# State-space heads of a hybrid diffusion step: one full-row selection matmul per direction, with the moving tile brought by DMA

## The chip, the cores and the metric

The kernel runs on one core of one Trainium2 chip. The metric is the device time of one execution in microseconds, as the median of several runs. All inputs, weights and results are f32 in HBM. The engines named below are PE (TensorE, matmuls), ACT (ScalarE), DVE (VectorE), POOL (GpSimd) and SP (SyncE, which here issues every DMA).

## What is computed

The reference is one inference step of a two-layer trunk, for 128 context tokens and 256 latent tokens. Layer 0 mixes tokens with a Fourier transform and with attention, layer 1 with a gated linear recurrence (RG-LRU) and with a state-space model of 16 heads (SSD). Each layer ends in a SwiGLU network. The change lies in the state-space heads. For each of two directions and each chunk of 128 tokens the reference computes

```python
acs = jnp.cumsum(dtc * A.reshape(G, Hg), axis=2)
diff = acs[:, :, :, None] - acs[:, :, None, :]
causal = jnp.tril(jnp.ones((Q, Q), dtype=bool))[:, :, None, None]
decay = jnp.exp(jnp.where(causal, diff, -jnp.inf))
cb = jnp.einsum("bcqgn,bckgn->bcqkg", Cc, Bc)
y_diag = jnp.einsum("bcqkg,bcqkgh,bckgh,bckghp->bcqghp", cb, decay, dtc, xc)
...
y_off = jnp.einsum("bcqgn,bcghpn,bcqgh->bcqghp", Cc, h_in, jnp.exp(acs))
```

So for each head, direction and chunk a 128 x 128 matrix exp(acs[q] - acs[k] + log dt[k]) is wanted, masked to one side of the diagonal. There are three chunks: one of context tokens and two of latent tokens.

## The kernel before

Activations lie with channels on partitions and tokens in the free dimension: 128 context tokens, two gap columns that carry the shift, and 256 latent tokens, 386 in all. Weights come from HBM in chunks of eight 128 x 128 blocks (`wr`, 512 KB, four buffers). ACT rounds a chunk to its high part (`wh`), DVE takes the rest (`wl`), and PE makes each product as three matmuls: high by high, high by low and low by high (`mm3`, line 622). The layers' stages follow each other: even mixer, network 0, odd mixer, network 1.

No engine's order is written by hand. All operations are recorded first; then a list scheduler (`schedule`, lines 308 to 456) gives each engine an order, with a cost for each instruction, the number of buffers of each pool, and a limit on how far ahead of the oldest unscheduled operation one may be taken. That limit is the first number of a row of `PARTS` (lines 213 to 218); the odd mixer is the third row. Since ACT, DVE, PE and SP each work through their order as it stands, a waiting instruction holds up all that stand behind it. Helpers record the operations, so that a profile shows lines 529 (ACT), 539 and 552 (DVE), 589 and 593 (PE) and 582 (SP) for nearly all of them, and tiles have to be told apart by name.

`odd_mixer` (line 1109) projects 27 tiles of 128 output channels from the normed input: 27 x 8 x 3 = 648 matmuls of 386 columns on `xh` and `xl`. The order of the tiles is written at line 1112; each is evacuated and worked on as it comes:

- `deltas` (line 1226) makes the step sizes `dt` and the cumulative sums `acs`, transposes `acs` and `nacs` (log dt - acs) to 32 rows (16 heads x 2 directions), and splits each with `both` into high and low parts, `rr` and `nrr`. In these 128-row tiles rows 0 to 63 and rows 64 to 127 hold the same numbers. It also makes `pick` (columns of an identity), `sel` and `ee` (exp(acs), high and low, 64 rows), and the two masks.
- `xs_tile` (line 1338) makes the heads' inputs `xt` and, scaled, `xw`; `states` (line 1368) makes the chunk states `Hc` and stores `news`.
- `ssd` (line 1389) runs twice after every second `xs` tile, for two heads each. For a head it fills one PSUM bank per direction: a matmul of 384 columns brings acs[q] to all 128 partitions, three matmuls of 128 columns add the key's own log dt - acs, and a matmul of 384 columns adds the mask. Direction 0 uses rows 0 to 63, direction 1 rows 64 to 127:

```python
                for d in range(2):
                    ds = slice(64 * d, 64 * d + 64)
                    r = S["pick"][ds, d * 16 + h:d * 16 + h + 1].to_broadcast([64, 128])
                    self.mm(q[d][:, :NC_], r, S["rr"][ds], True, False)
                    for c in range(3):
                        cc = slice(c * 128, (c + 1) * 128)
                        self.mm(q[d][:, cc], S["nrr"][ds, cc], r, False, False)
```

  ACT takes the exponential into `M` (32 in all), DVE adds the directions and multiplies by `cb`. One more matmul of 64 rows and 256 columns (`sel`, `ee`) gives the decay for the state's part, and DVE makes `exs` of it. `M` and `exs` then go through PE with `xt` and `Hc`, and `ysum` holds the head's output.
- `gated` (line 1454) takes SiLU of the `z` tiles (`zw`), multiplies, squares (`sq`) and sums (`ss`); `lru` and `lru_scan` do the recurrence, `gate` (line 1431) makes `gu` and the split pair `mh`, `ml`.

After the 27 tiles the norm of `ysum` is computed (matmuls on `ss`, then `rs`), and the output projection follows: 8 x 12 x 3 = 288 matmuls of 384 columns on `mh` and `ml`, whose first four of twelve row blocks come from `gate`. Exp and Tanh, SiLU and Tanh, GELU and Tanh, Sqrt, and Ln lie in different activation tables; ACT loads one (ACT_TABLE_LOAD) when the next function is not in the present table.

Of the kernel before, what the change touches and what calls it, by code (L numbers as in the profile page):

```python
# [9 lines left out]
F32 = mybir.dt.float32  # L10
F32R = mybir.dt.float32r
I32 = mybir.dt.int32
BF16 = mybir.dt.bfloat16
AF = mybir.ActivationFunctionType
ALU = mybir.AluOpType
# [9 lines left out]
NC_ = NP_ + NS_  # L25
# [45 lines left out]
def constants():  # L71
    c = np.zeros((128, NCON), np.float32)
    c[:, CO["ident"]] = np.eye(128)
    c[:, CO["ones"]] = 1.0
    h = np.arange(128)
    c[:, CO["halves"]][:, 32:34] = h[:, None] // 64 == np.arange(2)[None]

    c[:, CO["lo"]] = h[:, None] <= h[None]
    c[:, CO["up"]] = h[:, None] >= h[None]
    t = np.arange(NS_)  # L80
    pos = np.stack([t // 64, t % 64]).astype(np.float32)
    freqs = (np.float32(10000.0) ** (-np.arange(16, dtype=np.float32) / np.float32(16))).astype(np.float32)
    d = h % 64
    ang = pos[d // 32] * freqs[d % 16][:, None]
    sign = np.where(d % 32 < 16, -1.0, 1.0)[:, None]
    c[:, CO["cos"]] = np.cos(ang)
    c[:, CO["sin"]] = np.sin(ang) * sign
    a = 2 * np.pi * ((d[:, None] * d[None]) % 64) / 64
    same = (h[:, None] // 64) == (h[None] // 64)
    c[:, CO["dft64"]] = np.concatenate([np.where(same, np.cos(a), 0), np.where(same, np.sin(a), 0)], 1)  # L90
    a = 2 * np.pi * ((h[:, None] * h[None]) % 128) / 128
    s = 1 / math.sqrt(128 * 64)
    c[:, CO["dft128"]] = np.concatenate([np.cos(a) * s, -np.sin(a) * s], 1)
    a = 2 * np.pi * ((t[:, None] * t[None]) % 256) / 256
    s = 1 / math.sqrt(256 * 64)
    for k in range(2):
        c[:, CO["dft256" + "ac"[k]]] = np.cos(a[k * 128:(k + 1) * 128]) * s
        c[:, CO["dft256" + "bd"[k]]] = -np.sin(a[k * 128:(k + 1) * 128]) * s
    return c

# [97 lines left out]
class Recorder:  # L200
# [12 lines left out]
    PARTS = (  # L213
        (900, 10, 150, 0.8, 0.25, 60),
        (500, 12, 150, 0.4, 0.15, None),
        (900, 10, 150, 0.4, 0.25, 200),
        (500, 12, 150, 0.4, 0.15, None),
    )

# [239 lines left out]
class Kernel:  # L459
# [649 lines left out]
    def odd_mixer(self):  # L1109
# [114 lines left out]
        S = {}  # L1224

        def deltas(p):

            t = self.slot("dtT")
# [3 lines left out]
            q = self.bank()  # L1232
            for c in range(3):
                self.tp(q[:, c * 128:(c + 1) * 128], t[:, CH[c]:CH[c] + 128])
            v = self.tile("dv", 96, F32, "c")
# [6 lines left out]
            q = self.bank()  # L1242
# [5 lines left out]
            acs = self.tile("acs", 96, F32, "c")  # L1248
# [4 lines left out]
            et = self.tile("et", 96, F32, "c")  # L1253
            self.act(et, tot[:, 0:96], AF.Exp)
            q = self.bank()
            for c in range(3):
                self.tp(q[0:32, c * 128:(c + 1) * 128], acs[:, c * 32:(c + 1) * 32])
            def both(q):

                rr = self.slot("rr", NC_, F32R)  # L1260
                for z in range(2):
                    self.act(rr[64 * z:64 * z + 32], q[0:32, :NC_], AF.Copy)
                self.tt(rr[32:64], q[0:32, :NC_], rr[0:32].bitcast(F32), ALU.subtract)
                self.act(rr[96:128], rr[32:64].bitcast(F32), AF.Copy)
                return rr

            rr = both(q)
            er = self.slot("er", NC_)
            self.act(er[0:32], q[0:32, :NC_], AF.Exp)
            ee = self.slot("ee", NC_, F32R)  # L1270
            self.split_hl(ee[0:32], ee[32:64], er[0:32])

            nacs = self.tile("nacs", 96, F32, "c")
            self.ts(nacs, dt, 2.0 ** -126, ALU.max)
            self.act(nacs, nacs, AF.Ln)
            self.tt(nacs, nacs, acs, ALU.subtract)
            q = self.bank()
            for c in range(3):
                self.tp(q[0:32, c * 128:(c + 1) * 128], nacs[:, c * 32:(c + 1) * 32])
            nrr = both(q)  # L1280
            pick = self.slot("pick", 32, F32R)
            for z in range(4):
                zs = slice(32 * z, 32 * z + 32)
                self.act(pick[zs], self.ident[zs, zs], AF.Copy)

            sel = [self.tile("sel", 1024, F32R, "k") for _ in range(2)]
            for z in range(2):
                for d in range(2):
                    self.act(sel[z][0:64].split(8)[:, :, d * 64:d * 64 + 64],
                             pick[0:64, d * 16 + z * 8:d * 16 + z * 8 + 8].bitcast(F32).unsqueeze(2).to_broadcast([64, 8, 64]), AF.Copy)  # L1290

            mask = []
            for mk in ("lo", "up"):
# [2 lines left out]
                mask.append(t)  # L1296
            dd = self.tile("dd", 96, F32, "c")
            self.tt(dd, dt, de)
            S.update(dd=dd, nrr=nrr, et=et, rr=rr, ee=ee, pick=pick, sel=sel, mask=mask)

        def bc(i, p):
            y = conv(p, self.sm("csw")[:, (8 + i) * 4:(8 + i) * 4 + 4], self.sm("csb")[:, 8 + i:9 + i])
# [86 lines left out]
        def ssd(j):  # L1389

            o = self.bank()
            g = j // 4
            M, ex = {}, {}
            for hb in range(2):
                h = 2 * j + hb
                q = [self.bank() for _ in range(2)]
                for d in range(2):
                    ds = slice(64 * d, 64 * d + 64)
                    r = S["pick"][ds, d * 16 + h:d * 16 + h + 1].to_broadcast([64, 128])
                    self.mm(q[d][:, :NC_], r, S["rr"][ds], True, False)  # L1400
                    for c in range(3):
                        cc = slice(c * 128, (c + 1) * 128)
                        self.mm(q[d][:, cc], S["nrr"][ds, cc], r, False, False)
                for d in range(2):
                    self.mm(q[d][:, :NC_], self.identr, S["mask"][d], False, True)
                    m = self.slot("M", NC_)
                    self.act(m, q[d][:, :NC_], AF.Exp)
                    M[hb, d] = m
                self.tt(M[hb, 0], M[hb, 0], M[hb, 1], ALU.add)
                self.tt(M[hb, 0], M[hb, 0], S["cb"][g])  # L1410
                q = self.bank()
                self.mm(q[:, 0:256], S["sel"][h // 8][0:64, h % 8 * 128:h % 8 * 128 + 128], S["ee"][0:64, 128:384])
                ex[hb] = self.slot("exs", NS_)
                self.tt(ex[hb], q[:, 0:256], S["cs"][g])
            for c in range(3):
                cc = slice(c * 128, (c + 1) * 128)
                for hb in range(2):
                    self.mm(o[hb * 64:hb * 64 + 64, cc], xt[j][:, c * 128 + hb * 64:c * 128 + hb * 64 + 64], M[hb, 0][:, cc],
                            True, c == 0)
                if c:  # L1420
                    for hb in range(2):
                        h = 2 * j + hb
                        self.mm(o[hb * 64:hb * 64 + 64, cc], Hc[c - 1][:, h * 64:h * 64 + 64], ex[hb][:, (c - 1) * 128:c * 128], False, True)
            y = self.slot("ysum", NC_)
            for i in range(2):
                self.stt(y[:, CSEG[i]], ysum[j][:, SEG[i]], skip[:, j:j + 1], o[:, CSEG[i]], ALU.mult, ALU.add)
            ysum[j] = y
# [281 lines left out]
```

## Time and profile before

| | |
|---|---|
| median of 3 runs | 983.16 us (982.57 to 983.31) |
| the profiled execution | 981.94 us |
| its span | 980.2 us, 16154 instructions |
| mean granted TensorE clock | 0.994 |
| busy: PE, DVE, ACT, POOL | 98%, 75%, 51%, 0% of the span |
| DMA | 159.85 MB, mean 163 GB/s |

A group of instructions is shown as line, engine, operation, the tile written and the tiles read (buffer numbers left out), its shapes and its count, then its busy time and the mean of one, then the idle time of the engine just before it with what ended it. Matmuls overlap, so the time of one is longer than the distance between two starts; a PE that is shown as busy may be waiting inside its queue. PEclk is the clock that was granted to TensorE, 1.00 for 2.4 GHz and 0.50 for 1.2 GHz.

### The profile page before, as it was taken

The page shows a single profiled execution, that of the slowest core. Times are in us where ns is not written, and L with a number is a line of the kernel's source. Part 1 is how long each engine was busy: PE and PEld are TensorE (multiplying, and loading weights), DVE is VectorE, ACT ScalarE, POOL GpSimd, SP SyncE. Part 2 cuts the span into 40 slices and gives each one's busy share as a digit, 9 for nine tenths or more (in the row PEclk, how much of TensorE's full clock was granted, in tenths as well). Part 3 has the DMA queues.
Part 4 walks back from the last instruction along what each step waited for, and adds up shares of the span by engine and source line. Part 5 has one row for each costly group of instructions (what it writes and reads, how often), then busy time and mean ns, then how long its engine had stood idle before and what let it go on. Part 6 is the DMA issues. An engine that isn't in the chain of part 4 may idle for free.

```text
span 980.2 us, 16154 instructions
## 1 busy us (share of the span) xinstructions
PE 958.7 (98%) x6190; PEld 916.9 (94%) x6190; DVE 731.0 (75%) x1550; ACT 499.4 (51%) x949; POOL 4.3 (0%) x41
## 2 busy tenths in 40 slices
PE   6999999999999999999999999999999999999998
PEld 4987879999999999999997888899999999999998
DVE  3598765999999999996399799895889555553332
ACT  4569774544333442344278989774444433342221
POOL 0000000000000000000000000000000000000000
PEclk9999999999999999999999999899999999999999
DMA  9983524765666667744321222134643333333340
GB/s 358 362 325 106 180 87 144 286 215 189 214 222 214 217 218 247 253 146 146 127 87 50 80 82 86 50 108 135 242 161 129 129 129 123 116 127 129 131 155 16
DMA packets 47179, 159.85 MB, mean 163 GB/s; under 512 B 5376, under 2 KB 9216, under 8 KB 47104
## 3 DMA queue, kind: packets, MB, share of 16 engines
q1 hardware_dynamic: 47104, 158.84, 46.5%
q8 instruction: 48, 0.79, 0.3%
q14 instruction: 27, 0.22, 0.1%
HBM read 156.45 MB, written 2.37 MB: 162 GB/s over the span
## 4 chain that ended last, share of the span: by engine, by line
PE 87%; ACT 8%; DVE 2%; issue 1%; DMA 1%; SPq 0%; DVEq 0%; ACTq 0%
PE ps L589 85%; PE ps L593 2%; ACT wh L529 1%; DMA ar<-in_ada 1%; ACT L529 1%; ACT xw L529 1%; ACT kk L529 1%; ACT X L529 1%; ACT M L529 0%; SPq L582 0%; ACT cv L529 0%; ACT ex L529 0%; ACT kl L529 0%; ACT th L529 0%; ACT xt L529 0%
## 5 line engine op out<-in xcount | busy, mean ns | idle before, releaser
L529 ACT ACTIVATE wh<-wr 128x1024 fp32r<-128x1024 f32 x191 | 202.0, 1058 | 354.3 <-PE ps L589 242.7
L589 PE MATMUL ps<-xh,wh 128*128 128x386 f32 x1016 | 347.9, 343 | 2.2 <-ACT rstd L529 2.2
L589 PE MATMUL ps<-xl,wh 128*128 128x386 f32 x1016 | 347.7, 342 | 0.0
L589 PE MATMUL ps<-xh,wl 128*128 128x386 f32 x1016 | 346.2, 341 | 0.0
L539 DVE TENSOR_TENSOR wl<-wr,wh 128x1024 fp32r<-128x1024 f32 x191 | 233.2, 1221 | 112.5 <-ACT wh L529 108.4
L589 PEld LDWEIGHTS ps<-xh,wh 128*128 128x128 f32 x1016 | 192.5, 190 | 6.0 <-ACT rstd L529 2.8
L589 PEld LDWEIGHTS ps<-xl,wh 128*128 128x128 f32 x1016 | 192.4, 189 | 3.1 <-issue 2.1
L589 PEld LDWEIGHTS ps<-xh,wl 128*128 128x128 f32 x1016 | 192.2, 189 | 0.9 <-issue 0.3
L552 DVE SCALAR_TENSOR_TENSOR junk<-ar,scb 128x1024 bf16<-128x1024 f32 x112 | 136.5, 1219 | 3.0 <-DMA ar<-in_ada 1.4
L589 PE MATMUL ps<-gh,wh 128*128 128x384 f32 x352 | 118.7, 337 | 0.0
L589 PE MATMUL ps<-gh,wl 128*128 128x384 f32 x352 | 118.5, 337 | 0.0
L589 PE MATMUL ps<-gl,wh 128*128 128x384 f32 x352 | 118.5, 337 | 0.0
L539 DVE TENSOR_TENSOR ft<-ps,rstd 128x386 f32<-128x386 f32 x88 | 48.2, 558 | 52.7 <-PE ps L589 50.5
L589 PEld LDWEIGHTS ps<-gl,wh 128*128 128x128 f32 x352 | 66.1, 188 | 0.0
L589 PEld LDWEIGHTS ps<-gh,wl 128*128 128x128 f32 x352 | 66.1, 188 | 0.0
L589 PEld LDWEIGHTS ps<-gh,wh 128*128 128x128 f32 x352 | 66.1, 188 | 0.0
L589 PE MATMUL ps<-ml,wh 128*128 128x384 f32 x160 | 54.3, 339 | 0.0
L589 PE MATMUL ps<-mh,wl 128*128 128x384 f32 x160 | 54.1, 338 | 0.0
L589 PE MATMUL ps<-mh,wh 128*128 128x384 f32 x160 | 53.3, 339 | 0.0
L529 ACT ACTIVATE xh<-x,G 128x128 fp32r<-128x128 f32 x64 | 26.3, 446 | 23.9 <-DVE x L552 16.8
L529 ACT ACTIVATE gh<-fs 128x384 fp32r<-128x384 f32 x44 | 23.1, 525 | 25.8 <-DVE fs L552 25.7
L552 DVE SCALAR_TENSOR_TENSOR fs<-ft,fs 128x128 f32<-128x128 f32 x88 | 33.3, 414 | 3.7
(226 smaller groups left out, 1044.9 us busy)
## 6 DMA issues: line engine op xcount, KB each, us to landing
wr<-in_wst SPq DMA_DIRECT2D x191, 512.0 KB, 3.3
ar<-in_ada SPq DMA_DIRECT2D x96, 512.0 KB, 4.6
x<-in_x SPq DMA_DIRECT2D x4, 386.0 KB, 9.6
out_y<-x SPq DMA_DIRECT2D x8, 193.0 KB, 2.9
scb<-in_cond SPq DMA_DIRECT2D x2, 512.0 KB, 6.5
lw<-in_lru_w SPq DMA_DIRECT2D x2, 512.0 KB, 4.7
Hc<-in_h SPq DMA_DIRECT2D x2, 256.0 KB, 4.7
out_new_ssd<-news SPq DMA_DIRECT2D x4, 128.0 KB, 1.8
```

What stands on the lines that cost most here:

```text
L529: lambda: nc.scalar.activation(out=R(out), in_=R(in_), func=func, bias=R(bias), scale=R(scale), accum_out=R(accum_out)),
L539: self.dve(out, [a, b], out.free, lambda: nc.vector.tensor_tensor(out=R(out), in0=R(a), in1=R(b), op=op))
L552: lambda: nc.vector.scalar_tensor_tensor(out=R(out), in0=R(a), scalar=R(s), in1=R(b), op0=op0, op1=op1, accum_out=R(accum_out)),
L589: self.rec.add("PE", c / 1e3, [out], [lhsT, rhs], lambda: nc.tensor.matmul(R(out), R(lhsT), R(rhs), start=start, stop=stop), cols=cols)
L593: self.rec.add("PE", 0.109, [out], [in_, ident], lambda: nc.tensor.transpose(R(out), R(in_), R(ident)), cols=2 * in_.shape[0])
```

## The change

A table `selv` of 18 tiles of zeros and ones is made on the host. For a head, its tile `mvt` (128 x 384) is brought by DMA, and a second, small DMA puts four rows of `rr` (the head's cumulative sums: high and low part, both directions) into rows 48 to 51. ACT copies the whole to `mv` in the rounded type. The stationary tile `own` (one per direction) holds log dt - acs of all heads and chunks, high part in rows 0 to 47 and low part in rows 64 to 111, and ones in the rows of its direction's sums. One matmul of 128 rows and 384 columns per head and direction then does what four of 64 rows did. `ee` and `sel` are zero-filled to 128 rows, `rr` is kept once and not doubled, `nrr` is gone, and the scheduler's limit for the odd mixer goes from 900 to 500.

```diff
+def selectors():
+    s = np.zeros((18, 128, NC_), np.float32)
+    for h in range(16):
+        for c in range(3):
+            s[h, [c * 16 + h, 64 + c * 16 + h], c * 128:(c + 1) * 128] = 1.0
+    for d in range(2):
+        s[16 + d, [48 + d, 50 + d], 0:128] = 1.0
+    return s
...
     PARTS = (
         (900, 10, 150, 0.8, 0.25, 60),
         (500, 12, 150, 0.4, 0.15, None),
-        (900, 10, 150, 0.4, 0.25, 200),
+        (500, 10, 150, 0.4, 0.25, 200),
...
-            def both(q):
-
-                rr = self.slot("rr", NC_, F32R)
-                for z in range(2):
-                    self.act(rr[64 * z:64 * z + 32], q[0:32, :NC_], AF.Copy)
-                self.tt(rr[32:64], q[0:32, :NC_], rr[0:32].bitcast(F32), ALU.subtract)
-                self.act(rr[96:128], rr[32:64].bitcast(F32), AF.Copy)
-                return rr
-
-            rr = both(q)
+            rr = self.slot("rr", NC_, F32R)
+            self.act(rr[0:32], q[0:32, :NC_], AF.Copy)
+            self.tt(rr[32:64], q[0:32, :NC_], rr[0:32].bitcast(F32), ALU.subtract)
...
+            self.memset(ee[64:128].bitcast(F32), 0.0)
...
-            self.tt(nacs, nacs, acs, ALU.subtract)
+            steps = self.tile("steps", 96, F32, "c")
             q = self.bank()
-            for c in range(3):
-                self.tp(q[0:32, c * 128:(c + 1) * 128], nacs[:, c * 32:(c + 1) * 32])
-            nrr = both(q)
-            pick = self.slot("pick", 32, F32R)
-            for z in range(4):
+            own = []
+            for d in range(2):
+                v = steps[:, d * 48:d * 48 + 48]
+                ds = slice(d * 16, d * 16 + 16)
+                self.tt(v.split(3), nacs.split(3)[:, :, ds], acs.split(3)[:, :, ds], ALU.subtract)
+                self.tp(q[0:48, d * 128:(d + 1) * 128], v)
+
+                w, t = self.slot("ownt", 128), self.slot("own", 128, F32R)
+                self.dma(w, self.io["selv"][16 + d, :, 0:128])
+                self.act(t, w, AF.Copy)
+                self.act(t[0:48], q[0:48, d * 128:(d + 1) * 128], AF.Copy)
+                self.tt(t[64:112], q[0:48, d * 128:(d + 1) * 128], t[0:48].bitcast(F32), ALU.subtract)
+                own.append(t)
+            pick = self.slot("pick", 32)
+            for z in range(2):
...
             for z in range(2):
+                self.memset(sel[z][64:128].bitcast(F32), 0.0)
...
                 q = [self.bank() for _ in range(2)]
+
+                t, mv = self.slot("mvt", NC_), self.slot("mv", NC_, F32R)
+                self.dma(t, self.io["selv"][h])
+                self.dma(t[48:52], S["rr"].bitcast(F32)[h:64:16])
+                self.act(mv, t, AF.Copy)
                 for d in range(2):
-                    ds = slice(64 * d, 64 * d + 64)
-                    r = S["pick"][ds, d * 16 + h:d * 16 + h + 1].to_broadcast([64, 128])
-                    self.mm(q[d][:, :NC_], r, S["rr"][ds], True, False)
-                    for c in range(3):
-                        cc = slice(c * 128, (c + 1) * 128)
-                        self.mm(q[d][:, cc], S["nrr"][ds, cc], r, False, False)
+                    self.mm(q[d][:, :NC_], S["own"][d], mv, True, False)
...
-                self.mm(q[:, 0:256], S["sel"][h // 8][0:64, h % 8 * 128:h % 8 * 128 + 128], S["ee"][0:64, 128:384])
+                self.mm(q[:, 0:256], S["sel"][h // 8][:, h % 8 * 128:h % 8 * 128 + 128], S["ee"][:, 128:384])
```

The scheduler's new order shows at three places. The rows name line, operation, tile written and tiles read, and size of the output; PSUM banks are `ps`. The first place is PE at one head of the middle of the program; before:

```order
L589 MATMUL ps_6249<-rr_5808,pick_5208 128x384
L589 MATMUL ps_6251<-rr_5808,pick_5208 128x384
L589 MATMUL ps_6249<-pick_5208,rr_5821 128x128
L589 MATMUL ps_6251<-pick_5208,rr_5821 128x128
```

and now, with the masks and the decay selection behind:

```order
L602 MATMUL ps_6382<-mv_6176,own_5240 128x384
L602 MATMUL ps_6388<-mv_6176,own_5247 128x384
L602 MATMUL ps_6382<-mask_5212,identr_71 128x384
L602 MATMUL ps_6388<-mask_5242,identr_71 128x384
L602 MATMUL ps_6396<-ee_5024,sel_5007 128x256
```

The pair of 128-column matmuls stands three times for a head before (`rr_5821` is the tile that the code calls `nrr`), so that eight matmuls have become two.

The second place is SP at the first heads; before, behind the weight chunks that are loaded ahead:

```order
L582 DMA wr_5817<-in_wst 128x1024
L582 DMA wr_5888<-in_wst 128x1024
L582 DMA out_new_ssd<-news_6025 128x256
L582 DMA wr_6165<-in_wst 128x1024
L582 DMA wr_6196<-in_wst 128x1024
L582 DMA out_new_ssd<-news_6228 128x256
```

and now:

```order
L595 DMA wr_5828<-in_wst 128x1024
L595 DMA mvt_5201<-rr_5822 4x384
...
L595 DMA out_new_ssd<-news_6012 128x256
L595 DMA mvt_6027<-in_selv 128x384
L595 DMA mvt_6037<-in_selv 128x384
L595 DMA mvt_6027<-rr_5822 4x384
L595 DMA mvt_6089<-in_selv 128x384
L595 DMA mvt_6037<-rr_5822 4x384
L595 DMA mvt_6104<-in_selv 128x384
L595 DMA wr_6115<-in_wst 128x1024
L595 DMA mvt_6089<-rr_5822 4x384
L595 DMA mvt_6104<-rr_5822 4x384
```

The tables of the first eight heads are loaded earlier, between weight chunks, and their eight small copies stand in one row after the weights; those of the next four stand behind the store of `news`, with a weight chunk between them. The last four heads' come later in the same way.

The third place is ACT after the exponentials of the first heads; before, where the gating (`zw`) begins:

```order
L529 ACTIVATE M_6130<-ps_6039 128x384
L529 ACTIVATE wh_6135<-wr_5705 128x1024
L529 ACTIVATE X_5186<-X_5186 128x128
L529 ACTIVATE X_5186<-X_5186 128x256
L529 ACT_TABLE_LOAD
L529 ACTIVATE zw_6152<-zt_5583 128x128
```

and now:

```order
L542 ACTIVATE wh_6164<-wr_5719 128x1024
L542 ACTIVATE mv_6176<-mvt_6027 128x384
L542 ACTIVATE mv_6182<-mvt_6037 128x384
L542 ACTIVATE mv_6187<-mvt_6089 128x384
L542 ACTIVATE mv_6193<-mvt_6104 128x384
L542 ACTIVATE xt_6201<-ps_6185 128x384
```

The sixteen `zw` now stand in one stretch after the last `M`, where before twelve of them stood ahead of it; and the program's ACT_TABLE_LOADs have become 15 where there were 22.

## Rows read from the trace of the kernel before

**Rows 1.** Busy time by stage (stretch: length, then each engine busy, with instructions)

```profile
core 0: us, PE busy (x) PEld busy (x) DVE busy (x) ACT busy (x) POOL busy (x), PEclk, DMA share, GB/s
493.20:618.40 125.20, 121.06 (x801) 106.44 (x803) 114.55 (x274) 109.97 (x234) 0.00 (x0) 0.98 0.23 76
618.40:642.10 23.70, 23.70 (x144) 21.07 (x145) 19.86 (x42) 19.43 (x35) 0.10 (x1) 0.94 0.17 54
642.10:724.80 82.70, 82.70 (x476) 82.25 (x476) 66.57 (x141) 37.13 (x60) 0.00 (x0) 1.00 0.50 177
```

**Rows 2.** The chain that ended last, in order of time: start, length, what

```profile
213.31 278.91 PE ps L589 x1589
...
616.06 108.73 PE ps L589 x627
```

**Rows 3.** Timeline of PE: start, length, instruction; where the output projection begins

```profile
641.75 0.34 PE L589 MATMUL ps<-xl,wh 128*128 128x386 f32 x1
641.92 0.34 PE L589 MATMUL ps<-xh,wl 128*128 128x386 f32 x1
642.10 0.72 PE L589 MATMUL ps<-cons,ss 128*128 128x1 f32 x6
642.68 0.42 PE L589 MATMUL ps<-mh,wh 128*128 128x384 f32 x1
```

**Rows 4.** Timeline of PE at one head: its selection, then the decay's

```profile
546.54 0.44 PE L589 MATMUL ps<-rr,pick 64*128 64x384 f32 x2
546.82 0.44 PE L589 MATMUL ps<-pick,rr 64*128 64x128 f32 x6
547.10 0.33 PE L589 MATMUL ps<-ee,sel 64*128 64x256 f32 x1
```

**Rows 5.** Busy time by microsecond where the granted clock falls and rises

```profile
614.00:615.00 1.00, 1.00 (x7) 0.93 (x5) 0.91 (x4) 1.00 (x3) 0.00 (x0) 0.60 0.91 336
...
620.00:621.00 1.00, 1.00 (x4) 0.79 (x3) 0.23 (x1) 0.65 (x3) 0.00 (x0) 0.50 0.00 0
621.00:622.00 1.00, 1.00 (x7) 1.00 (x7) 0.95 (x3) 1.00 (x1) 0.00 (x0) 0.99 0.36 123
```

**Rows 6.** Groups of ACT from 493 to 643 us

```profile
L529 ACT ACTIVATE wh<-wr 128x1024 fp32r<-128x1024 f32 x20 | 21.0, 1051 | 4.9 <-PE ps L589 4.9
L529 ACT ACT_TABLE_LOAD x15 | 19.2, 1283 | 0.3
```

**Rows 7.** Timeline of ACT: copies like the new ones and those that go

```profile
513.95 1.96 ACT L529 ACTIVATE rr<-ps 32x384 fp32r<-32x384 f32 x4
516.68 0.94 ACT L529 ACTIVATE rr<-rr 32x384 fp32r<-32x384 f32 x2
...
655.27 1.58 ACT L529 ACTIVATE mh<-ysum 128x384 fp32r<-128x384 f32 x3 [0.69 <-DVE ysum L552]
```

**Rows 8.** Timelines of ACT and DVE where the first pair for the output projection is made

```profile
638.05 0.51 ACT L529 ACTIVATE mh<-gu 128x384 fp32r<-128x384 f32 x1
...
638.98 0.55 DVE L539 TENSOR_TENSOR ml<-gu,mh 128x384 fp32r<-128x384 f32 x1
```

**Rows 9.** DMA issues from 560 to 660 us: KB each, median us from issue to landing

```profile
out_new_ssd<-news SPq DMA_DIRECT2D x2, 128.0 KB, 2.1
out_new_lru<-finals SPq DMA_DIRECT2D x1, 4.0 KB, 2.9
```

**Rows 10.** Timelines of SP (an issue), then ACT (the work that will stand between)

```profile
546.84 0.34 SPq L582 DMA_DIRECT2D out_new_ssd<-news  x1
...
561.74 2.79 ACT L529 ACTIVATE M<-ps 128x384 f32<-128x384 f32 x7
...
568.12 1.07 ACT L529 ACTIVATE xw<-xt,dd 128x64 f32<-128x64 f32 x4
...
571.52 0.79 ACT L529 ACTIVATE X<-X 128x128 f32<-128x128 f32 x2
572.21 1.04 ACT L529 ACTIVATE wh<-wr 128x1024 fp32r<-128x1024 f32 x1
```

More of the change, by code (lines that the diff above doesn't have):

```diff
@@ L1287, in deltas @@
             for z in range(2):
+                self.memset(sel[z][64:128].bitcast(F32), 0.0)
                 for d in range(2):
                     self.act(sel[z][0:64].split(8)[:, :, d * 64:d * 64 + 64],
-                             pick[0:64, d * 16 + z * 8:d * 16 + z * 8 + 8].bitcast(F32).unsqueeze(2).to_broadcast([64, 8, 64]), AF.Copy)
+                             pick[0:64, d * 16 + z * 8:d * 16 + z * 8 + 8].unsqueeze(2).to_broadcast([64, 8, 64]), AF.Copy)
             mask = []
@@ L1298, in deltas @@
             self.tt(dd, dt, de)
-            S.update(dd=dd, nrr=nrr, et=et, rr=rr, ee=ee, pick=pick, sel=sel, mask=mask)
+            S.update(dd=dd, own=own, et=et, rr=rr, ee=ee, sel=sel, mask=mask)
         def bc(i, p):
@@ L1627 @@
         x=(128, KC, NT), cond=(2, D), smalls=(128, NSM), consts=(128, NCON), wst=(N_CHUNKS, 128, NBLK * 128),
-        ada=(96, 128, 1024), ck=(2, 128, 128), cv=(128, 256), lru_w=(128, 16, 128), h0=(128, 1024))
+        ada=(96, 128, 1024), selv=(18, 128, NC_), ck=(2, 128, 128), cv=(128, 256), lru_w=(128, 16, 128), h0=(128, 1024))
     outs = dict(y=(128, KC, NT), new_k=(128, 2, 128), new_v=(128, 2, 128), new_lru=(128, 8), new_ssd=(128, 1024))
@@ L1646 @@
     A["consts"][:] = constants()
+    A["selv"][:] = selectors()
     s = A["smalls"]
```

## The prediction

> **What bounds the kernel now.** I read the stages first, then the chain, then the timelines inside the one stage that the change touches. The chain of waits is PE alone for 278.91 us from 213.31 and again for 108.73 us from 616.06 [rows 2]; between 493 and 616 it breaks into short pieces on ACT, DVE and PE. So outside the odd mixer nothing that the change does can shorten the end, and inside it there are two halves. From 493.2 (its input is normed) to 618.4 (the last `M` has been made) ACT is busy for 109.97 of 125.20 us and DVE for 114.55, while the 121.06 of PE contain waits inside its queue [rows 1]: here the three engines hold each other. From about 621 on PE issues one matmul every 0.17 to 0.18 us [rows 3], and 476 of them fill 82.70 us from 642.10 on [rows 1]. The first matmul of the output projection starts at 642.68, directly behind the projection's last and the six on `ss` [rows 3]. Nothing behind this point changes, so the whole question is how much earlier it comes. PE reaches it at 642.1 by its own work. The other side of the door is ACT and DVE: the first pair `mh`, `ml` is made at 638.05 and 638.98, and so is there at 639.5 [rows 8]. They are only about 3 us ahead of PE. Whatever PE gains beyond that is given back unless ACT gains too.
>
> **The selection on PE.** For one head the eight half-row matmuls run from 546.54 to 547.10, where the next kind starts: 0.56 us [rows 4]. They are replaced by two of 128 rows and 384 columns, at the 0.175 us of a full matmul [rows 3]: 0.35 us. Sixteen heads: 16 x 0.21 = 3.4 us less PE work. Bounds: 0, if the eight cost no more than their columns, and 3.4; I take 3.4, since the row is of this very sequence. One transpose fewer (three of `nacs` become two of `steps`) is below 0.2 us. The decay's matmul gets 128 rows at unchanged 256 columns: I cost it at nothing, since the distance of two matmuls goes with columns in all rows above; if it cost a tenth of its 0.33 us [rows 4], that would be 0.5 us over the heads.
>
> The Trainium skill speaks against this term: TensorE: Matmul & The Clock Gate, Part 3 (packing small matmuls), says that matmuls on different row groups run side by side. By that rule the eight run as four pairs, 384 + 3 x 128 = 768 columns, the same as two full matmuls of 384, and the term would be 0. The trace agrees on the pairing, and not on the sum: 0.56 us against 0.35.
>
> **The clock.** In the microsecond from 614 the granted clock falls to half (1.2 GHz) and is back in that from 621 [rows 5]. Just before, PE had issued heads 12 to 15: mostly half-row selections, with a pause. At most 6.6 us at half speed have cost 3.3 us; as PE also waited for ACT there, I take 2.0. Ends: 0 (the dip comes again) and 3.3. That full-row matmuls keep the clock up is plausible and not shown by any row; a new dip elsewhere is the third rival.
>
> **ACT.** Added: 16 copies `mv` of 128 x 384 into the rounded type. The nearest rows are three `mh` copies of that shape, 1.58 us for three, and the two `rr` copies of 32 rows, 0.94 for two [rows 7]: 0.53 and 0.47 each, so 7.5 to 8.4; I take 7.8. Two small `own` copies add about 0.8, by the length of the `rr` copies; the full-width `own` copies and the zero fills on POOL fall into the network before, where PE alone is the chain. Removed: three of the four `rr` copies out of PSUM (1.96 for four) and both copies of `rr` [rows 7], 2.4 us. The new order loads an activation table seven times less: 7 x 1.283 = 9.0 us [rows 6]; all fifteen loads between 493 and 643 stand in the stretch at issue. Sum: 7.8 + 0.8 - 2.4 - 9.0 = -2.8 us for the stage.
>
> Where that falls matters more. By the new order twelve `zw` and six squares (18 x 0.4, the distance of two `M` [rows 10]), four weight copies (4 x 1.04 [rows 10]), one table load and some 5 us of the last heads' own inputs move behind the last `M`: about 18 us of ACT, and as much goes from ahead of it, the seven loads among that. The last head therefore comes much earlier, and ACT's work from there to the first `mh` grows from 15 us (of the 19.43 in rows 1 those ahead of 638.05) to 33, about as much as PE has left there: 168 projection matmuls where there were 96, x 0.175 = 29.5 us, and the last heads' products. Up to the first `mh` ACT's total work is then only about 0.7 us less than before, because work that stood behind that point has moved ahead of it. DVE loses one split of `rr` and gains two small ones of `own`: 0.
>
> **The queues.** SP gets 34 more issues at 0.34 us [rows 10], 12 us of a queue that mostly waits for buffers. The bytes, 16 x 197 KB, are nothing at a DMA share of 0.23 [rows 1]. The new waits are the matter. For heads 0 to 7 only the small copies are due; eight issues behind one another and a landing of 2.1 to 2.9 us [rows 9] end before ACT has done its other work there. For heads 8 to 11 the chain starts when ACT has made `news`: store, two table loads, a landing, small copy, a landing, so 0.34 x 4 + 2.1 + 2.5 = 6 us for the first, and about 10 for the fourth, which has a weight chunk and two more landings in front. Meanwhile ACT has 1.07 (`xw`) + 0.79 (`X`) + 4 `mv` at 0.5 + 2 x 1.04 (`wh`) + eight `M` at 0.4 [rows 10] = 9 us. That fits, with 3 us to spare for the first. The buffers of the later tables have to be free in time as well, which no row shows. I add 0, with 0 to 8 as ends.
>
> **The sum.** PE's side: 642.1 - 3.4 - 2.0 = 636.7. ACT and DVE's side: the first pair at 639.5 - 0.7 = 638.8. The later side decides: the projection starts some 3.8 us earlier. The profiled execution took 981.94 us, which gives 978.1; the median of the runs is 1.2 us higher, so 979.3 is forecast.
>
> **The rivals.** *Slower: the small copies are late.* ACT stands at `mv` while SP waits for a buffer or a landing; behind ACT's copy all `M` wait, and behind SP's the next weight chunks. It decides from a hold of more than 3 us in the chain of heads 8 to 11. With 4 us lost at each of the two later groups of four heads, the gain is gone and 4 us more: 987. For it: three dependent transfers replace none, on a queue that also carries `news` and weights. Against: SP is idle most of this time, and the first half of the heads is loaded ahead.
>
> *The tail becomes ACT's.* With 33 us behind the last `M`, three more microseconds of waiting there than the 4.3 that ACT has after 618.4 (23.70 - 19.43 [rows 1]) undo most of it: 982.
>
> *The clock falls in another stretch.* The heads now stand closer together, with few projection matmuls between them. Then the 2.0 are not won and up to 3.3 lost once: PE's side is 642.1 - 3.4 - 0 + 1.3 = 640, and the time 981 to 982.
>
> *The selection is worth nothing on PE*, if the pairs are as good as full rows, which also covers that the change does not do what it says: 642.1 - 2.0 = 640.1, and 981.2.
>
> *More is won.* ACT stood idle for 15.2 us of the 125.2 before the last `M` [rows 1], part of it waiting for PE (4.9 us at `wh` alone [rows 6]). If that shrinks by 4 us with the shorter selections, both sides move: 975.
>
> **How the numbers follow.** About 0.2%, 2 us, can be told from no change. Forecast 0.41; more won 0.14; small copies late 0.23; ACT's tail 0.10; clock elsewhere 0.08; no gain on PE 0.04. Faster by more than 0.2% are the first two and little of the others, 0.56; slower is the first rival, 0.23; the rest is 0.21. The range has to take in most of the slow rival and of the larger gain: 973 to 988; the forecast's own would be 976 to 981.
>
> **What would show it.** Right: table loads down by seven; the PE time of a head's two matmuls near 0.35 us; no granted clock of 0.5 from 493 to 643; the first `mh` matmul of the output projection 3 to 5 us earlier after the stage's start; ACT hardly waiting at `mv`. Wrong: ACT or PE waiting for the landing of the small copies, SP issuing weight chunks late so that ACT stands at `wh`, or a last `M` that is not at least 10 us earlier than before.

## The result, and the profile after

Four timed runs of each kernel on one chip give a median of 977.65 us (976.92 to 978.87) for the changed kernel and 982.87 us (982.43 to 983.31) for the one before: a ratio of 0.9948, 95% interval 0.9931 to 0.9965, or 5.2 us less. The forecast was 979.3, 3.9 us below the 983.16 that was known then. One kernel does not take the same time in every execution: of 57 executions of the kernel before that ran beside the experiments, 15 had a mean granted clock of 0.998 or more and took 979.2 to 980.1 us, and eleven had 0.991 and took 983.0 to 984.4, so that some 4 us of a difference can hang on whether the clock falls. All four executions of the changed kernel, at 0.992 to 0.996, lie below even the fastest of these. The profiled execution took 976.92 us, its span 974.8.

The page's first part, busy time by engine, of the changed kernel:

```profile
span 974.8 us, 16051 instructions
PE 950.2 (97%) x6093; PEld 911.3 (93%) x6093; DVE 729.8 (75%) x1552; ACT 494.5 (51%) x955; POOL 6.4 (1%) x44
```

Busy time by stage, columns as in [rows 1]; the cuts are again the stage's start, the last `M`, and the end of PE's own work (where the `ss` matmuls start):

```profile
493.60:600.10 106.50, 102.19 (x640) 90.15 (x641) 96.78 (x228) 90.31 (x201) 0.68 (x10) 1.00 0.26 89
600.10:632.60 32.50, 32.50 (x207) 30.23 (x206) 31.90 (x72) 30.27 (x63) 0.10 (x1) 1.00 0.26 86
632.60:719.00 86.40, 83.80 (x475) 83.39 (x475) 70.94 (x161) 41.11 (x71) 0.00 (x0) 0.98 0.47 171
```

The last `M` comes 18 us earlier than before, and what follows it has grown from 23.7 to 32.5 us, as the order said. PE's own work ends at 632.6 instead of 642.1. But PE then does nothing for 2.2 us. PE's timeline where the output projection begins, and ACT's beside it (compare [rows 3, 8]):

```profile
632.43 0.34 PE L602 MATMUL ps<-xh,wl 128*128 128x386 f32 x1
632.61 0.73 PE L602 MATMUL ps<-cons,ss 128*128 128x1 f32 x6
635.51 2.29 PE L602 MATMUL ps<-mh,wh 128*128 128x384 f32 x6 [2.18 <-ACT mh L542]
```

```profile
632.90 1.78 ACT L542 ACTIVATE gu<-gt 128x128 f32<-128x128 f32 x5
634.94 1.06 ACT L542 ACTIVATE mh<-gu 128x384 fp32r<-128x384 f32 x2 [0.26 <-DVE gu L552]
```

The other side of the door, the first `mh`, came from 638.05 to 634.94, and is now the later one. Directly behind PE's pause the granted clock falls to half; busy time by microsecond, the column before the last two is PEclk:

```profile
634.00:635.00 1.00, 0.00 (x0) 0.00 (x0) 1.00 (x4) 0.74 (x3) 0.00 (x0) 1.00 0.90 340
635.00:636.00 1.00, 0.48 (x1) 0.49 (x2) 1.00 (x4) 0.98 (x3) 0.00 (x0) 0.64 0.31 123
637.00:638.00 1.00, 1.00 (x5) 1.00 (x4) 1.00 (x5) 1.00 (x4) 0.00 (x0) 0.50 0.00 0
639.00:640.00 1.00, 1.00 (x7) 1.00 (x6) 0.93 (x10) 0.99 (x2) 0.00 (x0) 1.00 0.40 61
```

So of 9.5 us that PE gained, 7.2 reach the first `mh` matmul (642.68 to 635.51), some 1.5 go to the new dip (the busy share of each microsecond times what its clock is short of 1), and 5.4 remain in the span. The groups of ACT from 493 to 643 show the traded work (compare [rows 6]): six table loads and 7.7 us less in this stretch (the seventh stood behind 643), two `wh` more, sixteen `mv`, for which ACT never waited:

```profile
L542 ACT ACTIVATE wh<-wr 128x1024 fp32r<-128x1024 f32 x22 | 23.2, 1053 | 10.0 <-PE ps L602 9.4 <-ACT t L542 0.5
L542 ACT ACT_TABLE_LOAD x9 | 11.5, 1283 | 0.2
L542 ACT ACTIVATE mv<-mvt 128x384 fp32r<-128x384 f32 x16 | 7.2, 522 | 0.0
```

Busy time from the stage's start to the first `mh`, before and after, columns as above:

```profile
493.20:638.05 144.85, 140.71 (x919) 123.46 (x920) 130.76 (x308) 125.38 (x261) 0.10 (x1) 0.98 0.21 70
493.60:634.94 141.34, 135.43 (x851) 121.03 (x851) 131.02 (x306) 122.65 (x268) 0.78 (x11) 1.00 0.26 90
```

### The profile page after: what moved, and what is told of

Read it like the earlier page. It is cut to its first block, busy times and chain, and to the rows that moved or that the text cites. A ratio compares the mean times of both kernels' runs of the same rounds, so it can differ in the third digit from the quotient of the medians.

```text
span 974.8 us, 16051 instructions
## 1 busy us (share of the span) xinstructions
PE 950.2 (97%) x6093; PEld 911.3 (93%) x6093; DVE 729.8 (75%) x1552; ACT 494.5 (51%) x955; POOL 6.4 (1%) x44
## 4 chain that ended last, share of the span: by engine, by line
PE 81%; DVE 9%; ACT 6%; issue 2%; DMA 1%; SPq 0%; DVEq 0%; ACTq 0%
PE ps L602 80%; PE ps L606 1%; DVE wl L552 1%; DVE cv L565 1%; DMA ar<-in_ada 1%; DVE M L552 1%; DVE ly L571 1%; ACT kk L542 1%; ACT wh L542 1%; DVE Hc L552 1%; ACT th L542 0%; SPq L595 0%; DVE X L552 0%; ACT L542 0%; DVE ysum L565 0%
```

## The experiments

Ratios are to the kernel before, run beside each on the same chip; the columns behind the ratio, in us but for the loads, are each of one profiled execution. One table first, since most readings come back to it. "Selection" and "masks" are summed over the sixteen heads from PE's timeline: the distance from the start of each such matmul to the start of the next matmul of any kind, so waits and slow clock are in it. "PE" is the same over all matmuls from the stage's start to `ss`, which is the time that PE takes to get there, its waits included. "Clock" is the PE time lost to a clock under 0.97 from 490 to 665: the busy share of each microsecond times what the granted clock is short of 1. Loads are ACT's table loads from 493 to 655.

| kernel | ratio | PE | selection | masks | clock | loads | first `mh` matmul |
|---|---|---|---|---|---|---|---|
| before | 1 | 148.4 | 15.0 | 7.4 | 3.4 | 16 | 642.7 |
| changed | 0.9948 | 138.5 | 7.7 | 8.4 | 1.5 | 9 | 635.5 |
| limit alone | 1.0080 | 157.0 | 16.7 | 11.2 | 8.2 | 9 | 652.0 |
| selection alone | 1.0020 | 146.6 | 6.8 | 11.7 | 3.1 | 14 | 642.0 |
| changed, paired | 0.9922 | 134.1 | 5.9 | 5.8 | 1.7 | 9 | 631.0 |
| the same on half rows | 0.9949 | 138.3 | 8.8 | 7.8 | 3.1 | 9 | 635.4 |
| changed, paired, limit 900 | 0.9978 | 142.1 | 6.6 | 8.8 | 3.4 | 14 | 639.7 |
| before, grouped | 0.9949 | 142.6 | 10.7 | 9.3 | 0 | 13 | 636.8 |
| before, grouped, limit 500 | 1.0011 | 148.0 | 10.7 | 12.3 | 3.0 | 11 | 642.1 |

### The two halves of the change apart

```diff
-        (900, 10, 150, 0.4, 0.25, 200),
+        (500, 10, 150, 0.4, 0.25, 200),
```

in the kernel before, and the reverse in the changed one.

> The kernel before with the scheduler's limit for the odd mixer at 500 and nothing else; its order then loads an activation table 15 times, as the changed kernel does, where the kernel before loads 22. Theory A (both parts are needed, because the output projection waits for the later of PE's own work and of ACT's first pair mh, ml): ACT's side gains up to 7 x 1.28 = 9 us, but PE still issues the half-row selections, so that PE's side stays at 640 to 642 of the span: 0 to 2 us faster than before, ratio 0.998 to 1.000. Theory B (the limit carries the gain, the selection is worth nothing on PE): the whole 5.2 us, ratio 0.994 to 0.996. Theory C (the selection carries it): no change, ratio 0.999 to 1.001.

> The changed kernel with the limit back at 900; its order has 20 table loads, two fewer than the kernel before. Theory A: PE's side gains 3.4 us, but ACT gets 7.8 + 0.8 - 2.4 - 2 x 1.28 = 3.6 us more in the stage, so that ACT's side of the output projection comes later: 0 to 4 us slower than before, ratio 1.000 to 1.004. Theory B: ACT's 3.6 us more and no gain on PE, 2 to 4 us slower, ratio 1.002 to 1.004. Theory C: the whole gain, ratio 0.994 to 0.996. The matmul pair of a head should take 0.35 us by A and C, and 0.5 or more by B.

The limit alone: 990.2 us, ratio 1.0080 (1.0064 to 1.0097), worse than any theory had it. The selection alone: 983.69, 1.0020 (1.0010 to 1.0031), inside theory A's range and at the edge of B's. Theory B falls by the first run and C by both: neither half carries the gain, and the two together win although each alone loses. The limit alone has as few table loads as the changed kernel (9), and its first `mh` matmul comes 16.5 us later: the loads do not decide by themselves. What PE does meanwhile stands in busy time by stretch of the limit alone:

```profile
520.00:524.00 4.00, 2.46 (x16) 1.89 (x14) 3.63 (x8) 3.94 (x10) 0.00 (x0) 1.00 0.37 130
524.00:531.00 7.00, 5.97 (x26) 4.13 (x27) 6.97 (x18) 6.10 (x18) 0.14 (x2) 0.53 0.01 2
531.00:538.00 7.00, 5.52 (x62) 4.22 (x58) 6.86 (x20) 3.37 (x11) 0.14 (x2) 0.98 0.06 19
538.00:545.00 7.00, 7.00 (x26) 6.88 (x27) 3.60 (x8) 2.79 (x7) 0.00 (x0) 0.51 0.01 2
626.00:631.00 5.00, 4.36 (x15) 2.16 (x16) 3.49 (x8) 5.00 (x13) 0.00 (x0) 0.66 0.25 99
```

At the first heads PE is busy for 2.5 of 4 us, then runs seven at half clock, pauses again, and runs seven more at half clock: 8.2 us lost in this execution where the kernel before lost 3.4. That is only a part of it. PE takes 8.6 us longer up to `ss`, and among the six executions those with more clock are not the faster ones (988.9 us at 0.987, 990.7 at 0.991). What else makes this order slow was not taken apart.

### Copies on POOL, and the decay on half rows

```diff
-                self.act(mv, t, AF.Copy)
+                self.copy_pool(mv, t)
```

> The changed kernel with its sixteen copies mv made by POOL, which is idle, instead of ACT; every engine's order is otherwise that of the changed kernel, instruction by instruction. ACT has 7.2 us less between 522 and 600 of the span. If ACT's side (the first pair mh, ml) sets the start of the output projection in the changed kernel, as its wait of 2.2 us there says, the projection starts up to 2.3 us earlier, until PE's own work sets it: ratio to the kernel before 0.992 to 0.994. If DVE sets it (its instructions are the chain there), nothing changes: 0.9945 to 0.9955. If POOL's copy takes far longer than ACT's 0.52 us, the exponentials wait for it: slower than the changed kernel by up to 4 x (POOL's duration - 0.52).

979.68 us, 0.9978 (0.9967 to 0.9989): 2.7 us above the next kernel, which ran beside it and is as fast as the changed one, though ACT has 7 us less to do. PE still waits 2.2 us for `mh`. Taking the copies from ACT to POOL is a loss on balance. Whether 7 us off ACT are worth something by themselves this run cannot tell, since DVE and POOL slow each other at the same time. POOL's copies (shortest, median and longest in ns; first and last start), then DVE's timeline beside POOL's, in this kernel:

```profile
L594 POOL CAST mv<-mvt x16: 502/606/4000, 517.4 to 585.6; 128x384 fp32r<-128x384 f32 x16
```

```profile
518.36 0.28 DVE L552 TENSOR_TENSOR own<-ps,own 48x128 fp32r<-48x128 f32 x1
518.67 0.62 DVE L552 TENSOR_TENSOR xw<-xt,dd 128x128 f32<-128x128 f32 x1
519.30 0.63 DVE L552 TENSOR_TENSOR Hc<-Hc,et 64x256 f32<-64x256 f32 x1
```

```profile
517.41 2.24 POOL L594 CAST mv<-mvt 128x384 fp32r<-128x384 f32 x4 [62.96 <-DMA mvt<-rr]
```

and DVE in the changed kernel, the same three instructions:

```profile
518.98 0.28 DVE L552 TENSOR_TENSOR own<-ps,own 48x128 fp32r<-48x128 f32 x1
519.30 0.29 DVE L552 TENSOR_TENSOR xw<-xt,dd 128x128 f32<-128x128 f32 x1
519.60 0.42 DVE L552 TENSOR_TENSOR Hc<-Hc,et 64x256 f32<-64x256 f32 x1
```

While POOL copies, `xw` takes 0.62 instead of 0.29 us and `Hc` 0.63 instead of 0.42; `own`, which reads one of its operands from PSUM, stays at 0.28. It goes the other way too: the copy of 4.00 us lies from 537.19 to 541.19, where DVE, up to 540.7, runs one instruction on two SBUF operands after the other without a gap. The Trainium skill says that POOL shares its way into SBUF with DVE and meets DVE instructions that read two operands there (GPSIMD Engine Reference, Key points); the rows agree. How much of the 2.7 us this accounts for was not measured.

```diff
-                self.mm(q[:, 0:256], S["sel"][h // 8][:, h % 8 * 128:h % 8 * 128 + 128], S["ee"][:, 128:384])
+                self.mm(q[:, 0:256], S["sel"][h // 8][:, h % 8 * 128:h % 8 * 128 + 128], S["ee"][:, 128:384], half=True)
```

With `half=True` the matmul is planned as before and issued on rows 0 to 63 of both operands.

> The changed kernel with the decay's matmul (sel, ee) back on 64 rows, the order of every engine as in the changed kernel. The rows 64 to 127 it leaves out are zeros. If a matmul's time goes with its columns alone, no change: 0.9938 to 0.9958 of the kernel before, that is within 0.1% of the changed kernel. If the half rows cost PE time (the engine changes between full-row and half-row matmuls) or pull the clock down, it is slower than the changed kernel: 16 x 0.1 = 1.6 us for the first, up to 3 us for the second.

977.03 us, 0.9950 (0.9934 to 0.9966): no change. The decay's part of the change is worth nothing either way, as forecast.

### A head's two matmuls together, on full and on half rows

```diff
-                for d in range(2):
-                    self.mm(q[d][:, :NC_], S["own"][d], mv, True, False)
+                self.mm_both([q[d][:, :NC_] for d in range(2)], S["own"], mv, False)
```

One recorded step issues both matmuls; with True it issues four of 64 rows instead, from an `own` whose parts for direction d both lie in rows 64d to 64d + 63.

> The changed kernel with the two selection matmuls of a head recorded as one step, so that they always stand side by side in PE's order; nothing is computed otherwise. It is the control for the next kernel. Expected by every theory: as the changed kernel within its spread, 0.993 to 0.997 of the kernel before; the pair at 0.35 us.

> The control with each full-row matmul of the selection split into two of 64 rows and 384 columns: direction 0 on rows 0 to 63, direction 1 on rows 64 to 127, high parts first, then low parts, interleaved as in the kernel before; a second small copy brings the sums to rows 112 to 115. Columns and order of PE otherwise as in the control. Theory A (half rows cost PE time and lower the granted clock when heads stand close together, which is why the limit of 500 alone lost 8 us): four matmuls of a head take 0.45 to 0.56 us, stretches at a granted clock of 0.5 appear between 520 and 545, and the time is 3 to 9 us above the control, ratio to before 0.998 to 1.004. Theory B (half-row pairs are as good as full rows, and the loss of the limit alone came from its order): within 0.15% of the control, 0.994 to 0.997, no clock of 0.5 in the heads. Between them, PE time without a dip: +1 to +2 us over the control.

The control was meant to be neutral and was not: 973.34 us, 0.9922 (0.9906 to 0.9938), the fastest kernel of the study that computes everything (its interval and the changed kernel's just meet; they did not run in one set; the changed kernel without its `cb` products, below, ran beside it and took 976.61). In the changed kernel the scheduler puts other work between the two matmuls in seven of sixteen heads, and PE waits 2.1 us before `mv` matmuls, mostly for DVE's `exs` (none in the control, which waits 1.1 us for `exs` elsewhere). Selection and masks together take 11.7 us instead of 16.1. The half rows cost 3.3 us over their control, 976.60 us, 0.9949 (0.9932 to 0.9966). ACT waits 0.2 us at `mv` there, so that the second small copy is not what costs it. PE's timeline of the control, then of the half rows, near 535 us:

```profile
534.36 0.52 PE L613 MATMUL ps<-mv,own 128*128 128x384 f32 x2
534.71 0.51 PE L602 MATMUL ps<-mask,identr 128*128 128x384 f32 x2
535.06 0.51 PE L613 MATMUL ps<-mv,own 128*128 128x384 f32 x2
```

```profile
536.05 0.34 PE L606 MATMUL ps<-xh,wl 128*128 128x386 f32 x1
536.32 0.62 PE L617 MATMUL ps<-mv,own 64*128 64x384 f32 x4
536.87 0.62 PE L606 MATMUL ps<-mask,identr 128*128 128x384 f32 x2
537.42 0.62 PE L617 MATMUL ps<-mv,own 64*128 64x384 f32 x4
```

On full rows selection and masks follow at 0.35 us each. With half rows the four take 0.55, and so do the two masks behind them, although nothing about the masks differs. The pairs do run side by side (4 x 384 columns in 0.55 us, where full matmuls take 0.175 for each 384), but each passage between full and half rows takes extra: 0.27 us from the `xh,wl` to the first half-row matmul, where full follows full at 0.175. The Trainium skill names this (TensorEngine Tiling (Array Packing), Key Properties: a change of the tiling mode drains the engine), and the 0.1 us extra at each passage agrees with it. Summed over the heads it is 2.9 us of selection and 2.0 of masks. Theory A's price was right and its clock was not: the clock falls from 634 to 641, behind PE's pause at the output projection, and not in the heads.

### What sets the pace of the stage

```diff
-                self.tt(M[hb, 0], M[hb, 0], S["cb"][g])
+                self.dve(M[hb, 0], [M[hb, 0], S["cb"][g]], NC_, lambda: None)
```

> The changed kernel, in the order of the changed kernel, without DVE's sixteen multiplications of M by cb (0.554 us each, 8.9 us of DVE), so that the product C B is left out of the heads' own-chunk part. If DVE is what sets the pace from 493 to the start of the output projection (it is busy for 97 to 99 of 100 us there, and taking 7.2 us off ACT won nothing), the first mh matmul comes at least 2.3 us earlier, up to PE's own work at 632.9, and PE's waits for exs go: 2 to 4 us below the changed kernel, ratio 0.990 to 0.993. If ACT or PE sets it, within 1 us of the changed kernel, 0.994 to 0.996.

976.61 us, 0.9953 (0.9936 to 0.9970): no change, with 8.9 us less on DVE. The first `mh` matmul comes 0.8 us earlier. DVE does not set the pace in the heads.

```diff
-                self.tt(ss, ss, q, ALU.add)
+                self.dve(ss, [ss, q], NC_, lambda: None)
```

in the paired control, so that the work goes from the stretch behind the last head:

> The control without DVE's seven additions to ss (0.55 us each, 0.47 apart, 3.3 us of DVE between 615 and 625), so that the norm's sum covers one of eight tiles; order as in the control. In the control DVE is busy all of 600 to 631 and ACT 9.9 of each 10 us, while PE waits 3.6 us for the first pair mh, ml. If DVE sets that end of the stretch, the first mh matmul comes 1.5 to 3.3 us earlier and the drop of the clock at 632 to 635 goes: ratio to the kernel before 0.987 to 0.991. If ACT sets it, no change: 0.991 to 0.993.

972.72 us, 0.9917 (0.9896 to 0.9937): no change, and the first `mh` matmul comes at 631.2 where the control has 631.0. Busy time from 600 to 631 of the control, then without the additions:

```profile
600.00:631.00 31.00, 28.24 (x186) 25.89 (x184) 30.64 (x75) 30.25 (x64) 0.10 (x1) 1.00 0.27 84
```

```profile
600.00:631.00 31.00, 28.67 (x187) 26.31 (x185) 28.64 (x69) 30.34 (x65) 0.10 (x1) 1.00 0.29 92
```

DVE falls from 30.6 to 28.6 us; ACT stays at 30.3 and runs without a gap into the `mh` that PE waits for (ACT's timeline without the additions):

```profile
627.01 0.66 ACT L542 ACTIVATE xh<-mod 128x2 fp32r<-128x2 f32 x6
627.67 1.28 ACT L542 ACT_TABLE_LOAD   x1
628.97 1.78 ACT L542 ACTIVATE gu<-gt 128x128 f32<-128x128 f32 x5
630.65 0.92 ACT L542 ACTIVATE mh<-gu 128x384 fp32r<-128x384 f32 x2
```

So behind the last head it is ACT's queue that holds the projection, and not DVE's. ACT's work was not taken away there, so this rests on the gapless queue and on DVE's failure to matter.

### The small copies

```diff
-                self.dma(t[48:52], S["rr"].bitcast(F32)[h:64:16])
+                self.dma(t[48:52], S["rr"].bitcast(F32)[h:64:16], 2)
```

> The changed kernel with each small copy of a head's sums issued twice in a row, order otherwise that of the changed kernel: 16 issues of 0.34 us more on SP, four of them in each of the two later chains, and a second landing that mv has to wait for. If the small copies are hidden with some 3 us to spare, as reckoned, no change: 0.994 to 0.996. If they are close to the path, mv comes later by 0.34 to 1.4 us at heads 8 to 11 and again at 12 to 15, and the time is 1 to 3 us above the changed kernel: 0.996 to 0.998.

990.01 us, 1.0091 (1.0074 to 1.0108): some 13 us slower than the changed kernel, far outside both theories. The reckoning by issues was the wrong one. SP's timeline of the first eight heads' copies, in the changed kernel and then with two each; ACT's group and SP's waits of the latter:

```profile
515.73 4.46 SPq L595 DMA_DIRECT2D mvt<-rr  x8
```

```profile
515.57 19.15 SPq L595 DMA_DIRECT2D mvt<-rr  x16
```

```profile
L542 ACT ACTIVATE mv<-mvt 128x384 fp32r<-128x384 f32 x16 | 7.8, 519 | 11.3 <-DMA mvt<-rr 10.9 <-ACT mv L542 0.5
```

```profile
SPq L595 <- DMA mvt<-rr: 21.0, 16, 2.4
```

The second copy writes the rows of the first, and the program lets SP issue it only when the first has landed. So SP waits up to 2.4 us each time, and everything behind it on SP stands too: `news` leaves at 534.76 instead of 527.54. ACT waits 10.9 us at `mv` and the clock falls at 525 to 532, at 553 to 556 and again at 648 to 651, behind PE's pause. That is the slow rival of the prediction, brought about by the second copies: its mechanism is real, and in the changed kernel it simply does not set in.

### The same grouping without the change

```diff
-                for d in range(2):
-                    ...
-                    self.mm(q[d][:, :NC_], r, S["rr"][ds], True, False)
-                    ...
+                self.mm_head(q, S["pick"], S["rr"], S["nrr"], h)
```

in the kernel before: one step issues the eight half-row matmuls, directions in turn.

> The kernel before with the limit at 500, as in the run of the limit alone, but with the eight half-row matmuls of a head recorded as one step, so that they stand together in PE's order. 17 table loads. Theory A (the limit alone lost 8 us because the half-row pieces of several heads were spread over PE's order, each waiting for its bank, with 20 us at a granted clock of 0.5; half rows as such cost 0.31 us of a head): no clock of 0.5 between 520 and 545; against the control with full rows 16 x 0.31 = 5 us more on PE, no copies and tables to load: ratio to the kernel before 0.995 to 0.999. Theory B (heads that stand close together on half rows lower the clock however they are ordered): stretches at 0.5 again, 1.004 to 1.010.

> The kernel before with the eight matmuls of a head recorded as one step and nothing else; 19 table loads, three fewer than before. If the order of a head's own matmuls is worth as much here as it was from the changed kernel to the control (4 us), 0.995 to 0.997; if only the three loads count, 3.8 us of ACT on one side of the projection's start, of which PE's side lets about 2 us through, 0.998 to 1.000.

> The control (full-row selection, the two matmuls of a head as one step) with the limit back at 900: 20 table loads where the control has 15. If the limit works through ACT's loads, ACT's side of the projection's start comes up to 5 x 1.28 = 6.4 us later than in the control: ratio to the kernel before 0.996 to 0.999. If the limit only mattered through the order of PE's pieces, as in the control: 0.991 to 0.994.

Grouping alone, limit 900: 976.44 us, 0.9949 (0.9932 to 0.9967), the whole gain of the change, without its tables, copies or full rows: the same instructions in another order, in which the last `M` comes at 602.9 and three table loads fewer are needed. At a mean granted clock of 0.998 the kernel before takes 979.4 to 980.1 us and this one 976.2 to 976.5, so that some 3 of the 6 us are there without any difference in clock. With the limit at 500: 982.48, 1.0011 (1.0000 to 1.0022), between the two theories. The paired full rows at 900: 979.62, 0.9978 (0.9966 to 0.9990), in the range of the theory of the loads. But its first `mh` matmul comes 8.7 us later than in the control, where the loads could make at most 6.4, and PE's own work ends 9.3 later, so the order of PE counts as well. PE's timeline of the grouped kernel before, limit 900, at one head, and where its projection begins:

```profile
536.21 0.44 PE L601 MATMUL ps<-rr,pick 64*128 64x384 f32 x2
536.49 0.44 PE L601 MATMUL ps<-pick,rr 64*128 64x128 f32 x6
536.87 0.63 PE L589 MATMUL ps<-mask,identr 128*128 128x384 f32 x2
...
636.26 0.73 PE L589 MATMUL ps<-cons,ss 128*128 128x1 f32 x6
636.85 0.42 PE L589 MATMUL ps<-mh,wh 128*128 128x384 f32 x1
```

The eight take 0.66 us, nearly twice a full-row pair, yet no microsecond of this execution from 490 to 665 has a lowered clock, and PE does not wait for `mh`: here PE's own work decides.

What in the grouping brings the new order was not separated. To the scheduler the eight matmuls stood at 0.176 us each, on 64 rows; the one step stands at 0.35 us and, by the tiles it names, on 128 rows. So it changed the planned price and the planned rows together with the grouping. The pair of full-row matmuls, 2 x 0.176 us, keeps its price and rows when it is grouped, so there the grouping alone changed.

So three things together make the ratio, and their effects are not sums: full rows are worth 10.7 - 5.9 = 4.8 us of selection on PE; grouping, 0.26 to 0.7%; and the limit helps full rows (0.9978 to 0.9922) but harms half rows (0.9949 to 1.0011). At 900 the grouped half rows even beat the paired full rows by 3.2 us, although these have 4.1 us less selection. In the profiled execution at 500 the grouped half rows have PE waiting 3.2 us for an `M`, and then 3.0 us lost to a clock of 0.5 from 600 to 608. But that does not explain their loss: four other executions with a mean clock of 0.998 took 982.1 to 982.4 us, no less than those at 0.994 (982.4 to 982.9). Why the order comes out well for the one and not for the other stays open.

## Why the prediction was right, and where its steps were not

The sign, the place and the rough size were right: everything happened ahead of the output projection, and the later of two sides decided. The sizes of both sides were not.

- **Selection on PE, forecast -3.4.** The pair does take 0.35 us where nothing stands between. But selection fell by 7.3 us in sum. The failing step is that the half-row sequence was priced by itself: in the kernel before the pieces of a head are spread over PE's order with waits between (15.0 us, 0.94 a head, where [rows 4] show 0.56 for a compact one). Full-row matmuls behind half-row ones come later too, which the forecast did not cost (masks 7.8 us on half rows against 5.8 in their control); in the changed kernel itself that was not won, its masks rose from 7.4 to 8.4. The rule weighed there, from the Trainium skill (TensorE: Matmul & The Clock Gate, Part 3), that matmuls on different row groups run side by side, would have made the term 0; half rows against full rows in the same order cost 3.3 us.
- **The clock, forecast -2.0 and no new dip.** The dip at 614 to 621 is not in the changed kernel's profile (3.4 us by rows, the forecast's upper end 3.3), and a new one of 1.5 us stands at 635, behind PE's wait. The forecast took the old dip as fixed, but the kernel before has executions at 0.998 that are 3 us faster, with hardly room for it. The step failed in saying that none would come before 643; the rival that it falls elsewhere was in part true.
- **ACT, forecast -2.8 for the stage, -0.7 up to `mh`.** Loads -7.7 (forecast -9.0; one of the seven was counted in the wrong stretch), `mv` 7.2 (7.8). Up to the first `mh` ACT's busy time went from 125.4 to 122.7 us, -2.7 where -0.7 was reckoned, and it idled 0.8 us less; so this side came 3.1 us earlier and not 0.7. Reckoning the moved work from both ends of an order lost two microseconds. It was this side that decided, as forecast.
- **DVE, 0**: right, and the runs without `cb` and `ss` show that up to 8.9 us would not have mattered.
- **SP, +0 of 0 to 8**: right. ACT never waited at `mv`. The margin was given as 3 us; with SP held 7 us at the store of `news`, and again at the later copies, 13 us were lost.
- **The sum.** Sides of 636.7 and 638.8 were forecast, 632.6 and 635.5 (with PE's start on `mh`) measured: 3 to 4 us earlier each. That the result lies only 1.7 us from the forecast is luck: both sides were off by more, and the new dip gave some of it back.

What the forecast had least in view is that the same gain was to be had by order alone. It took the new order as a given consequence of the limit. The runs show that another order of the old matmuls is worth as much, that the selection alone loses 0.2%, and that the limit alone loses 0.8%.

## What to carry to other kernels

Before replacing small matmuls by larger ones, issue them as one block and measure that: a scheduler that may put other work between the pieces of a head can cost as much as the pieces, and issuing them as one step gave 0.5% here (the planner also took that step for a cheaper one). A change of a planner's limit and a change of what it plans have to be tested in all four combinations, since here each alone lost (0.8% and 0.2%) and both together won 0.5%. And where PE pauses, look whether half clock follows and count it with the pause: 1.5 us behind the 2.2 us here, none behind the same pause in the profiled execution with POOL's copies.

## What the runs showed of the hardware that was not expected

- Half-row matmuls delay the full-row ones behind them: a mask pair takes 0.55 us between half-row blocks and 0.35 between full-row ones.
- POOL's copies of 128 x 384 (median 0.61 us) and DVE's instructions on two SBUF operands slow each other: such an instruction took 0.62 us instead of 0.29, and one of the copies 4.00. A DVE instruction with a PSUM operand kept its 0.28.
- Where the program makes an issue wait for the DMA before it to land, the queue behind stands too, up to 2.4 us each: sixteen issues took 19.15 us where eight without such a wait took 4.46.
